# A seven-product block scheme in part of the down projections of a two-layer decoder trunk, on one core

## The chip, the core and the metric

The kernel runs on one core of a Trainium2 chip. The core has five engines that work side by side and meet only at semaphores: TensorE multiplies matrices (PE in the profile; PEld is its weight load), VectorE (DVE) and ScalarE (ACT) work elementwise, GpSimd (POOL) does some elementwise work, and SyncE (SP) starts the DMA transfers. Each engine takes its instructions in a fixed order, so an instruction that waits holds back all that stand behind it on the same engine. The metric is the time of one execution on the device, in microseconds (us), as a median over runs.

## The reference

The trunk has two residual layers, each a mixer and a gated MLP. Only the MLP (`conv_ffn`) matters here, and it runs twice:

```python
def conv_ffn(h, w_up, conv_w, conv_b, w_down):
    u = causal_dwconv(h @ w_up, conv_w, conv_b)
    gate, val = jnp.split(u, 2, axis=-1)
    return (jax.nn.silu(gate) * val) @ w_down
```

`h` is 512 tokens by 1024 channels, the inner width is 2816, all in float32. The down projection, `@ w_down`, is a product of 512 by 2816 with 2816 by 1024. Its result is added to the residual stream `x`.

## The kernel before

Activations lie transposed: channels on the 128 partitions, 512 tokens along the row. A float32 product is made of three products of a shorter float format (`F32R`): every operand is split into a high and a low part, and `products` (L155) issues, for each 128 by 128 block of weights, three matmuls of 512 columns into one PSUM bank: high by high (L159), high by low (L160), low by high (L161). Each matmul loads its 128 by 128 weights first (PEld).

`load` (L151) brings weights in: a DMA from SP's queue into a tile `raw`, ACT's copy into the high part `wh` (L139), DVE's subtraction into the low part `wl` (L144). Each of the three has three buffers, taken in turn. So a DMA waits until the `wl` of three loads earlier is made, and ACT's `wh` waits until TensorE is done with the load of three earlier.

`ffn` first runs the up projection (44 tiles; each ends in a few DVE and ACT operations, and the last of them is the low part `al` of the MLP's activation, L167), and keeps the activation as 22 tiles `ah` and `al` of 128 channels by 512 tokens. The down projection then makes the 8 output tiles one after another: for each `n`, three loads (8, 8 and 6 blocks of `k`), 66 matmuls, and `residual` (L217), in which DVE adds the bank to `x` (L219). In the first MLP, `residual` goes on with the next layer's norm (`Normed.add`: ACT's high part, DVE's low part, a square and a sum); in the second, it starts the DMA of the result. `Normed` keeps its parts in two large tiles, `xh` and `xl`, which the up projection reads.

The order on each engine is set by a scheduler when the program is built: it places the operations by its own estimate of when each can start, and the order is then fixed.

## Time and profile before

| what | value |
|---|---|
| median of 3 runs (lowest, highest) | 1125.85 us (1125.61, 1126.47) |
| the profiled execution's own time | 1128.6 us |
| its span, first to last instruction | 1126.8 us |
| granted clock of TensorE, mean | 0.988 of full speed |
| busy share of the span: PE, PEld, DVE, ACT, POOL | 97%, 78%, 66%, 45%, 14% |
| first down projection | 452.1 to 571.8 us of the span |
| second down projection | 1002.9 to 1122.6 us of the span |

The busy share counts any time in which an engine has an instruction under way. A matmul's duration covers its way through the pipeline, so matmuls overlap; what one costs in a row of many is the distance between two starts. Times in the rows further below are counted from the span's start.

### The profile page before, as it was taken

To read this page: it belongs to the slowest core of one execution; us is meant where nothing else is said; L and a number is where in the kernel's file an instruction comes from. 1 tells how busy PE (TensorE), PEld (TensorE's weight loads), DVE (VectorE), ACT (ScalarE), POOL (GpSimd) and SP (SyncE) were. 2 spreads that over 40 slices of the span, in tenths; PEclk is the share of its full clock that TensorE was granted. 3 is DMA by queue.
4 is the path that set the end of the run, shared out by engine and by line. 5 is a ranking of instruction groups with operands and counts; after the bars stand their busy time and mean duration, and the time that the engine had idled before them with its cause. 6 is when DMAs were issued, how large, how long until landed. Compare 5 with 4: busy or idle time off the path is not lost.

```text
span 1126.8 us, 12788 instructions
## 1 busy us (share of the span) xinstructions
PE 1089.6 (97%) x4898; PEld 875.4 (78%) x4898; DVE 748.7 (66%) x1052; ACT 508.0 (45%) x710; POOL 153.4 (14%) x131
## 2 busy tenths in 40 slices
PE   9989989999999999999999997799999999999998
PEld 7777767888888888888877762588888888888886
DVE  6888975677777777333369998776777777762221
ACT  6667644454444444322247444554444444441210
POOL 0132340000000000000039896000000000000000
PEclk9999999999999999999999998899999999999999
DMA  6311125223322223333334536132332233333340
GB/s 216 109 46 38 32 70 168 94 94 96 105 99 94 94 94 92 100 94 94 108 99 132 165 91 157 45 114 94 101 104 94 94 94 98 104 89 107 118 122 19
DMA packets 37406, 111.96 MB, mean 99 GB/s; under 512 B 4192, under 2 KB 4832, under 8 KB 37344
## 3 DMA queue, kind: packets, MB, share of 16 engines
q1 hardware_dynamic: 37344, 111.14, 32.0%
q8 instruction: 38, 0.62, 0.2%
q14 instruction: 24, 0.20, 0.1%
HBM read 107.18 MB, written 3.94 MB: 99 GB/s over the span
## 4 chain that ended last, share of the span: by engine, by line
PE 80%; DVE 9%; POOL 4%; ACT 3%; issue 2%; DMA 1%; SPq 0%; POOLq 0%; ACTq 0%; DVEq 0%
PE bank L159 25%; PE bank L161 25%; PE bank L160 25%; POOL y L754 3%; DVE bank L770 1%; ACT tap L751 1%; PE bank L724 1%; ACT wh L139 1%; DVE wl L144 1%; PE bank L894 1%; PE bank L895 1%; DVE u L696 1%; DMA stack<-d 1%; DVE fold L177 1%; DVE pl L167 0%
## 5 line engine op out<-in xcount | busy, mean ns | idle before, releaser
L159 PE MATMUL bank<-xh,wh 128*128 128x512 f32 x936 | 370.0, 396 | 1.6 <-ACT wh L257 1.5
L160 PE MATMUL bank<-xl,wh 128*128 128x512 f32 x936 | 366.2, 391 | 0.0
L161 PE MATMUL bank<-xh,wl 128*128 128x512 f32 x936 | 366.2, 391 | 0.0
L139 ACT ACTIVATE wh<-raw 128x1024 fp32r<-128x1024 f32 (+2 forms) x186 | 190.2, 1025 | 279.5 <-PE bank L160 236.7
L144 DVE TENSOR_TENSOR wl<-raw,wh 128x1024 fp32r<-128x1024 f32 (+2 forms) x175 | 210.6, 1205 | 143.8 <-ACT wh L139 141.9
L159 PEld LDWEIGHTS bank<-xh,wh 128*128 128x128 f32 x936 | 176.7, 189 | 42.6 <-issue 3.1
L161 PEld LDWEIGHTS bank<-xh,wl 128*128 128x128 f32 x936 | 176.3, 188 | 37.9 <-issue 0.7
L160 PEld LDWEIGHTS bank<-xl,wh 128*128 128x128 f32 x936 | 176.6, 189 | 36.8 <-issue 1.4
L159 PE MATMUL bank<-ah,wh 128*128 128x512 f32 x352 | 136.9, 389 | 0.0
L160 PE MATMUL bank<-al,wh 128*128 128x512 f32 x352 | 136.9, 389 | 0.0
L161 PE MATMUL bank<-ah,wl 128*128 128x512 f32 x352 | 136.9, 389 | 0.0
L931 DVE SCALAR_TENSOR_TENSOR y<-u,pt,y 128x511 f32<-128x511 f32 (+1 forms) x176 | 131.6, 748 | 7.7 <-ACT y L928 4.6
L926 DVE TENSOR_TENSOR u<-bank,rstd 128x512 f32<-128x512 f32 x88 | 60.5, 688 | 79.2 <-PE bank L161 79.2
L754 POOL TENSOR_TENSOR y<-y,tap 128x512 f32<-128x512 f32 x54 | 81.5, 1511 | 10.8 <-ACT tap L751 7.3
L166 ACT ACTIVATE ah<-y 128x512 fp32r<-128x512 f32 x44 | 27.8, 632 | 114.9 <-DVE y L936 114.9
L161 PEld LDWEIGHTS bank<-ah,wl 128*128 128x128 f32 x352 | 66.1, 188 | 13.8
L160 PEld LDWEIGHTS bank<-al,wh 128*128 128x128 f32 x352 | 66.1, 188 | 13.8
L159 PEld LDWEIGHTS bank<-ah,wh 128*128 128x128 f32 x352 | 66.1, 188 | 13.6
L928 ACT ACTIVATE y<-u,pt 128x512 f32<-128x512 f32 x88 | 71.3, 810 | 4.8 <-DVE u L926 3.8
L935 ACT ACTIVATE y<-y 128x512 f32<-128x512 f32 x44 | 27.8, 633 | 82.8 <-DVE y L931 82.8
L219 DVE TENSOR_TENSOR xr<-bank,xr 128x512 f32<-128x512 f32 x32 | 22.0, 690 | 63.0 <-PE bank L161 63.0
L770 DVE SCALAR_TENSOR_TENSOR bank<-u,pt,bank 128x512 f32<-128x512 f32 x79 | 56.8, 747 | 0.7
(194 smaller groups left out, 1072.5 us busy)
## 6 DMA issues: line engine op xcount, KB each, us to landing
raw<-in_w_up SPq DMA_DIRECT2D x88, 512.0 KB, 3.3
raw<-in_w_down SPq DMA_DIRECT2D x32, 512.0 KB, 3.5
raw<-in_w_pw SPq DMA_DIRECT2D x24, 512.0 KB, 3.4
stack<-d SPq DMA_DIRECT2D x28, 256.0 KB, 5.1
raw<-in_w_down SPq DMA_DIRECT2D x16, 384.0 KB, 3.2
xr<-in_x SPq DMA_DIRECT2D x16, 256.0 KB, 5.4
raw<-in_w_out SPq DMA_DIRECT2D x8, 512.0 KB, 3.6
raw<-in_w_qk SPq DMA_DIRECT2D x6, 512.0 KB, 3.4
```

The source lines that it names most:

```text
L139: S.activation(out=wh, in_=raw, func=AF.Copy)
L144: on.tensor_tensor(out=wl, in0=raw, in1=wh.bitcast(F32), op=ALU.subtract)
L159: PE.matmul(acc, lhsT=ah, rhs=bh, start=(first and i == 0), stop=False)
L160: PE.matmul(acc, lhsT=ah, rhs=bl, start=False, stop=False)
L161: PE.matmul(acc, lhsT=al, rhs=bh, start=False, stop=(last and i == n - 1))
L166: S.activation(out=h, in_=src, func=AF.Copy)
L754: G.tensor_tensor(out=mine["y2"], in0=mine["y2"], in1=mine[s], op=ALU.add)
L770: V.scalar_tensor_tensor(out=acc, in0=shifted(s), scalar=wcol(s), in1=acc, op0=ALU.mult, op1=ALU.add)
L926: V.tensor_tensor(out=u, in0=acc, in1=nrm.r, op=ALU.mult)
L928: S.activation(out=y, in_=u, func=AF.Identity, scale=col("cv_w", 3 * ct + 2), bias=col("cv_b", ct))
L931: V.scalar_tensor_tensor(out=y[:, s:], in0=u[:, 0:T - s], scalar=col("cv_w", 3 * ct + 2 - s), in1=y[:, s:], op0=ALU.mult, op1=ALU.add)
L935: S.activation(out=ys[0], in_=ys[0], func=AF.Silu)
```

## The change

Four blocks of weights, two neighbouring `k` and two neighbouring outputs `n`, form a 2 by 2 block matrix; the two `k` tiles of the activation, cut into two halves of 256 tokens, form another. Their product takes eight block products of 256 columns in the plain way. The change makes it of seven (Winograd's form of Strassen's scheme), from sums and differences of the blocks. It does so for the first six of the eleven pairs of `k`, and not for every pair of outputs: `USED` says that output pairs 0 to 3 use it for 2, 4, 6 and 6 pairs of `k`, so 18 of the 44 in each down projection. The rest (`plain`) is as before, in loads of 2, 4, 6 or 8 blocks.

- `differences(f)`, once for each of the six pairs of `k`: GpSimd adds the high and low parts of two activation tiles back together (L971, twice), DVE makes four half-width sums and differences (L973 to L976), and ACT and DVE split them (L166, L167 on 1024 columns). They share one tile `r`, of which there is one buffer. Four of the results lie in the space of `xh` and `xl`, two in a new tile.
- `fast(p, f, ...)`: a DMA of four blocks, three DVE operations for four more (L985, L987, L988), the split of seven blocks (896 columns: L139, L144), and 21 matmuls of 256 columns, into the two banks of the outputs and two more, `e`.
- `combine(p, e)`: once for each pair of outputs, ACT and DVE work out what the banks `e` add to the two outputs (L1017 to L1029), in a tile `qd` that takes the same single buffer as `r`.
- In each pair of outputs the loads stand in this order: plain ones, the fast ones, `combine`, differences still to be made, the last plain ones, the additions to `x` (L1060). Three differences are made ahead of output pair 0, two behind its `combine`, and one behind that of pair 1. The next norm takes its first six tiles when the fourth fast product of the last pair is done.

The core of the diff (`up` holds the up projection as it was):

```diff
+    FAST = tuple(range(6))
+    USED = (2, 4, 6, 6)
+    HT = T // 2
+    halves = [slice(0, HT), slice(HT, T)]
     def ffn(layer, nrm, next_norm):
-        with tc.tile_pool(name="ffn", bufs=1) as fp, tc.tile_pool(name="ffn2", bufs=2) as f2:
+        with tc.tile_pool(name="ffn", bufs=1) as fp:
             ah = fp.tile([P, FT, T], F32R, name="ah")
             al = fp.tile([P, FT, T], F32R, name="al")
...
-            nxt = next_norm(f2)
-            for n in range(KT):
+            with tc.tile_pool(name="ffn2", bufs=2) as f2:
+                up(layer, nrm, ah, al, f2)
+            with tc.tile_pool(name="ffnt", bufs=1) as ft:
+                return down(layer, ah, al, ft, next_norm)
...
-                for k0 in range(0, FT, KT):
-                    kk = min(KT, FT - k0)
-                    wh, wl = load(w_down[layer, n][:, k0:k0 + kk], [kk, P])
-                    products(acc, [(wh[:, k], wl[:, k], ah[:, k0 + k], al[:, k0 + k])
-                                   for k in range(kk)], first=(k0 == 0), last=(k0 + kk == FT))
-                residual(acc, n, nxt)
-            if nxt is not None:
-                nxt.finish()
-            return nxt
...
+    def down(layer, ah, al, ft, next_norm):
+        near = [per.tile([P, 4, 4, HT], F32R, tag=t, name=f"t_{t}") for t in ("xh", "xl")]
+        far = [ft.tile([P, 2, 4, HT], F32R, name=f"t_far{i}") for i in range(2)]
+        parts_of = [[t[:, f] for t in near] if f < 4 else [t[:, f - 4] for t in far]
+                    for f in range(len(FAST))]
+        def differences(f):
+            k = 2 * FAST[f]
+            r = ft.tile([P, 6, HT], F32, tag="r", name="r")
+            flat = r.rearrange("p a t -> p (a t)")
+            for i, on in ((0, G), (1, G)):
+                on.tensor_tensor(out=flat[:, i * T:(i + 1) * T], in0=ah[:, k + i].bitcast(F32),
+                                 in1=al[:, k + i].bitcast(F32), op=ALU.add)
+            V.tensor_tensor(out=r[:, 4:6], in0=r[:, 0:1].to_broadcast([P, 2, HT]), in1=r[:, 1:3],
+                            op=ALU.subtract)
+            V.tensor_tensor(out=r[:, 2], in0=r[:, 2], in1=r[:, 4], op=ALU.subtract)
+            V.tensor_tensor(out=r[:, 3], in0=r[:, 3], in1=r[:, 2], op=ALU.subtract)
+            split(r[:, 2:6], *parts_of[f])
+        def fast(p, f, o, e, first_e, last_e):
+            j = FAST[f]
+            raw = wp.tile([P, 8, P], F32, tag="wr", name="raw", bufs=3)
+            nc.sync.dma_start(out=raw[:, 0:4].rearrange("p (n k) c -> p n k c", n=2),
+                              in_=w_down[layer, 2 * p:2 * p + 2, :, 2 * j:2 * j + 2].rearrange(
+                                  "n p k c -> p n k c"))
+            V.tensor_tensor(out=raw[:, 4:6], in0=raw[:, 0:1].to_broadcast([P, 2, P]),
+                            in1=raw[:, 1:3], op=ALU.add)
+            V.tensor_tensor(out=raw[:, 6], in0=raw[:, 4], in1=raw[:, 2], op=ALU.add)
+            V.tensor_tensor(out=raw[:, 7], in0=raw[:, 6], in1=raw[:, 3], op=ALU.add)
+            wh, wl = load_parts(raw[:, 1:8], [7, P])
+            th, tl = parts_of[f]
+            def b(k, half):
+                return ah[:, 2 * j + k, halves[half]], al[:, 2 * j + k, halves[half]]
+            def t(i):
+                return th[:, i], tl[:, i]
+            for i, (bh, bl), acc, half in (
+                    (1, b(0, 1), e[0], 0), (5, t(0), e[0], 1), (3, t(2), e[1], 0),
+                    (4, t(3), e[1], 1), (6, b(1, 0), o[1], 0), (2, b(1, 1), o[1], 1),
+                    (0, t(1), o[0], 1)):
+                products(acc[:, halves[half]], [(wh[:, i], wl[:, i], bh, bl)],
+                         first_e and i in (1, 3), last_e and i in (5, 4))
+        def plain(p, ks, o, first, last):
+            for n in range(2):
+                w = load(w_down[layer, 2 * p + n][:, ks[0]:ks[-1] + 1], [len(ks), P])
+                products(o[n], [(w[0][:, i], w[1][:, i], ah[:, k], al[:, k])
+                                for i, k in enumerate(ks)], first, last)
+        def combine(p, e):
+            x0, x1 = res["x"][:, 2 * p], res["x"][:, 2 * p + 1]
+            r = ft.tile([P, 6, HT], F32, tag="r", name="qd")
+            q, d = r[:, 0:2].rearrange("p a t -> p (a t)"), r[:, 2:4]
+            S.activation(out=q[:, halves[0]], in_=e[0][:, halves[0]], func=AF.Copy)
+            V.tensor_tensor(out=q[:, halves[1]], in0=e[0][:, halves[1]], in1=q[:, halves[0]],
+                            op=ALU.subtract)
+            V.tensor_tensor(out=d, in0=e[1].rearrange("p (a t) -> p a t", a=2),
+                            in1=q[:, halves[1]].rearrange("p (a t) -> p a t", a=1).to_broadcast(
+                                [P, 2, HT]), op=ALU.add)
+            V.tensor_tensor(out=x1[:, halves[1]], in0=x1[:, halves[1]], in1=q[:, halves[0]],
+                            op=ALU.add)
+            V.tensor_tensor(out=x1[:, halves[0]], in0=x1[:, halves[0]], in1=d[:, 0],
+                            op=ALU.subtract)
+            x0h = x0.rearrange("p (a t) -> p a t", a=2)
+            V.tensor_tensor(out=x0h, in0=x0h, in1=d[:, 1:2].to_broadcast([P, 2, HT]), op=ALU.add)
+            V.tensor_tensor(out=x0[:, halves[0]], in0=e[1][:, halves[0]], in1=x0[:, halves[0]],
+                            op=ALU.add)
+        for f in range(USED[0] + 1):
+            differences(f)
+        nxt, made, todo = None, USED[0] + 1, []
+        for p in range(KT // 2):
+            o = [bank(next(turn)) for _ in range(2)]
+            e = [bank(next(turn)) for _ in range(2)]
+            use = list(range(USED[p]))
+            ks = [k for k in range(FT) if k // 2 not in [FAST[f] for f in use]]
+            cuts = ((0, 8, 14, 18), (0, 6, 14), (0, 2, 10), (0, 2, 10))[p]
+            blocks = [ks[a:b] for a, b in zip(cuts, cuts[1:])]
+            for i, ks in enumerate(blocks[:-1]):
+                plain(p, ks, o, i == 0, False)
+            for f in use:
+                fast(p, f, o, e, f == 0, f == use[-1])
+                if p == KT // 2 - 1 and f == 3:
+                    nxt = next_norm and next_norm()
+                    for n in range(2 * p if nxt else 0):
+                        nxt.add(n)
+            combine(p, e)
+            if made < len(FAST) and p < 2:
+                to = (USED[1] + 1, len(FAST))[p]
+                for f in range(made, to):
+                    differences(f)
+                made = to
+            plain(p, blocks[-1], o, False, True)
+            for n in range(2 * p, 2 * p + 2):
+                xn = res["x"][:, n]
+                V.tensor_tensor(out=xn, in0=o[n % 2], in1=xn, op=ALU.add)
+                if next_norm is None:
+                    nc.sync.dma_start(out=out[:, n], in_=xn)
+                elif nxt is not None:
+                    nxt.add(n)
+        if nxt is not None:
+            nxt.finish()
+        return nxt
```

On TensorE a load of 8 blocks of one output reads, in the order before, as three matmuls for each `k` (`ah`, `al`: the activation; `wh`, `wl`: the weights):

```order
L159 MATMUL bank<-ah,wh 128x512
L160 MATMUL bank<-al,wh 128x512
L161 MATMUL bank<-ah,wl 128x512
L159 MATMUL bank<-ah,wh 128x512
L160 MATMUL bank<-al,wh 128x512
L161 MATMUL bank<-ah,wl 128x512
```

The same engine now, at the end of the first fast product of a pair (`t_xh`, `t_xl` are the parts of the differences):

```order
L159 MATMUL bank<-t_xh,wh 128x256
L160 MATMUL bank<-t_xl,wh 128x256
L161 MATMUL bank<-t_xh,wl 128x256
L159 MATMUL bank<-ah,wh 128x256
L160 MATMUL bank<-al,wh 128x256
L161 MATMUL bank<-ah,wl 128x256
L159 MATMUL bank<-ah,wh 128x256
L160 MATMUL bank<-al,wh 128x256
L161 MATMUL bank<-ah,wl 128x256
L159 MATMUL bank<-t_xh,wh 128x256
L160 MATMUL bank<-t_xl,wh 128x256
L161 MATMUL bank<-t_xh,wl 128x256
```

So 12 matmuls of 512 columns have become 21 of 256, each with a weight load of its own.

On DVE, at the seam of the first up and down projection, the order before was this (`u`, `y`, `al`: the end of the up projection; `wl`: low parts of weights for the down projection):

```order
L926 TENSOR_TENSOR u_3745<-bank_3720,rstd_1803 128x512
L144 TENSOR_TENSOR wl_3824<-raw_3820,wh_3822 128x768
L931 SCALAR_TENSOR_TENSOR y_3747<-u_3745,pt_67,y_3747 128x511
L931 SCALAR_TENSOR_TENSOR y_3747<-u_3745,pt_67,y_3747 128x510
L936 TENSOR_TENSOR y_3710<-y_3710,y_3747 128x512
L167 TENSOR_TENSOR al_2038<-y_3710,ah_2037 128x512
L144 TENSOR_TENSOR wl_3853<-raw_3849,wh_3851 128x1024
L144 TENSOR_TENSOR wl_3883<-raw_3879,wh_3881 128x1024
L219 TENSOR_TENSOR xr_1791<-bank_3759,xr_1791 128x512
```

And now, from the same place on (`raw` of 256 or 128 columns: the sums of weights; `r`, `t_xl`: the first differences; 896 columns: the low parts of a fast product's weights):

```order
L956 TENSOR_TENSOR y_3710<-y_3710,y_3747 128x512
L985 TENSOR_TENSOR raw_3929<-raw_3929 128x256
L167 TENSOR_TENSOR al_2035<-y_3710,ah_2034 128x512
L987 TENSOR_TENSOR raw_3929<-raw_3929 128x128
L988 TENSOR_TENSOR raw_3929<-raw_3929 128x128
L144 TENSOR_TENSOR wl_3879<-raw_3875,wh_3877 128x768
L973 TENSOR_TENSOR r_3763<-r_3763 128x512
L975 TENSOR_TENSOR r_3763<-r_3763 128x256
L976 TENSOR_TENSOR r_3763<-r_3763 128x256
L167 TENSOR_TENSOR t_xl_3760<-r_3763,t_xh_3759 128x1024
L144 TENSOR_TENSOR wl_3906<-raw_3899,wh_3904 128x896
L973 TENSOR_TENSOR r_3771<-r_3771 128x512
```

The differences stand in the same queue as the low parts of the weights; POOL's two additions for each stand in POOL's own queue, the first behind the `al` shown here.

The third place is DVE ahead of the first fast product of output pair 1, where there was only the plain sequence of `wl` and `xr`:

```order
L144 TENSOR_TENSOR wl_4053<-raw_4049,wh_4051 128x768
L976 TENSOR_TENSOR r_3967<-r_3967 128x256
L985 TENSOR_TENSOR raw_4073<-raw_4073 128x256
L985 TENSOR_TENSOR raw_4103<-raw_4103 128x256
L1060 TENSOR_TENSOR xr_1791<-bank_3788,xr_1791 128x512
L167 TENSOR_TENSOR t_xl_3760<-r_3967,t_xh_3759 128x1024
```

```order
L987 TENSOR_TENSOR raw_4103<-raw_4103 128x128
L988 TENSOR_TENSOR raw_4073<-raw_4073 128x128
L988 TENSOR_TENSOR raw_4103<-raw_4103 128x128
L985 TENSOR_TENSOR raw_4133<-raw_4133 128x256
L973 TENSOR_TENSOR r_3975<-r_3975 128x512
L144 TENSOR_TENSOR wl_4080<-raw_4073,wh_4078 128x896
```

The fifth differences (`r_3975`, not needed before output pair 2) stand ahead of `wl_4080`, the low parts of the weights of pair 1's first fast product.

## Rows read from the trace of the kernel before

**Rows 1.** Two down projections by stage: busy time (and instructions) of each engine, PEclk.

```profile
452.10:571.80 119.70, 119.70 (x530) 99.10 (x528) 43.64 (x49) 33.96 (x41) 0.00 (x0) 1.00 0.32 95
1002.90:1122.60 119.70, 119.70 (x529) 98.89 (x527) 32.95 (x34) 23.04 (x24) 0.00 (x0) 1.00 0.30 92
```

**Rows 2.** Timeline of PE at two 256-column triples of the attention.

```profile
81.84 0.28 PE L159 MATMUL bank<-ph,vhl 128*128 128x256 f32 x1
...
82.20 0.22 PE L159 MATMUL bank<-ph,vhl 128*128 128x128 f32 x1
...
145.70 0.28 PE L159 MATMUL bank<-ph,vhl 128*128 128x256 f32 x1
...
146.05 0.22 PE L159 MATMUL bank<-ph,vhl 128*128 128x128 f32 x1
```

**Rows 3.** Groups of DVE, shapes apart: busy, mean ns, idle before.

```profile
L144 DVE TENSOR_TENSOR wl<-raw,wh 128x1024 fp32r<-128x1024 f32 x155 | 192.6, 1245 | 143.8 <-ACT wh L139 141.9
L144 DVE TENSOR_TENSOR wl<-raw,wh 128x768 fp32r<-128x768 f32 x16 | 15.3, 959 | 0.0
L219 DVE TENSOR_TENSOR xr<-bank,xr 128x512 f32<-128x512 f32 x32 | 22.0, 690 | 63.0 <-PE bank L161 63.0
L167 DVE TENSOR_TENSOR pl<-bank,ph 128x256 fp32r<-128x256 f32 x8 | 3.3, 411 | 0.0
L167 DVE TENSOR_TENSOR pl<-bank,ph 128x128 fp32r<-128x128 f32 x8 | 2.3, 284 | 0.7 <-ACT ph L166 0.7
```

**Rows 4.** Groups of ACT, shapes apart.

```profile
L139 ACT ACTIVATE wh<-raw 128x1024 fp32r<-128x1024 f32 x166 | 175.4, 1060 | 233.7 <-PE bank L160 191.1 <-issue 33.7 <-PE bank L898 5.1
L166 ACT ACTIVATE ph<-bank 128x256 fp32r<-128x256 f32 x8 | 3.0, 376 | 1.0 <-PE bank L534 0.9
```

**Rows 5.** Timeline of DVE at the end of the first up projection.

```profile
455.46 0.69 DVE L936 TENSOR_TENSOR y<-y 128x512 f32<-128x512 f32 x1
456.86 0.69 DVE L167 TENSOR_TENSOR al<-y,ah 128x512 fp32r<-128x512 f32 x1 [0.70 <-ACT ah L166]
```

**Rows 6.** POOL's additions of 512 columns, by line and tile: min, median, max ns.

```profile
L754 POOL TENSOR_TENSOR y<-y,tap x54: 1264/1298/2375, 590.1 to 692.1; 128x512 f32<-128x512 f32 x54
L422 POOL TENSOR_TENSOR us<-us x6: 1039/1040/1277, 139.0 to 160.9; 128x512 f32<-128x512 f32 x6
```

**Rows 7.** DVE and POOL at the same time: timelines of two stretches, and line L696.

```profile
598.09 2.09 DVE L144 TENSOR_TENSOR wl<-raw,wh 128x1024 fp32r<-128x1024 f32 x1 [0.64 <-ACT wh L139]
599.18 3.86 POOL L754 TENSOR_TENSOR y<-y,tap 128x512 f32<-128x512 f32 x2
601.81 0.74 DVE L770 SCALAR_TENSOR_TENSOR bank<-u,pt,bank 128x512 f32<-128x512 f32 x1
...
146.11 2.79 POOL L144 TENSOR_TENSOR wl<-raw,wh 128x1024 fp32r<-128x1024 f32 x1
146.69 2.23 DVE L429 TENSOR_TENSOR mx<-us,pt 128x7 f32<-128x7 f32 x1
...
L696 DVE TENSOR_TENSOR u<-ab x8: 692/1772/1784, 587.8 to 681.7; 128x512 f32<-128x512 f32 x8
```

**Rows 8.** DMA issues: KB each, us from issue to landing.

```profile
raw<-in_w_down SPq DMA_DIRECT2D x16, 384.0 KB, 3.2
...
w<-in_w_dw SPq DMA_DIRECT2D x1, 128.0 KB, 2.3
```

**Rows 9.** A standstill of PE and the stretch after it: timeline, then its window.

```profile
73.18 0.66 PE L534 MATMUL bank<-ident,p 128*128 128x128 f32 x2 [2.73 <-DVE p L526]
...
74.07 0.63 PE L160 MATMUL bank<-xl,wh 128*128 128x512 f32 x1
74.50 0.63 PE L161 MATMUL bank<-xh,wl 128*128 128x512 f32 x1
...
73.20:76.60 3.40, 3.40 (x10) 2.78 (x11) 3.27 (x8) 2.94 (x7) 0.00 (x0) 0.53 0.00 0
```

More of the change, by code (lines that the diff above doesn't have):

```diff
@@ L910, in odd_layer @@
             return nxt
+    FAST = tuple(range(6))
+    USED = (2, 4, 6, 6)
+    HT = T // 2
+    halves = [slice(0, HT), slice(HT, T)]
     def ffn(layer, nrm, next_norm):
-        with tc.tile_pool(name="ffn", bufs=1) as fp, tc.tile_pool(name="ffn2", bufs=2) as f2:
+        with tc.tile_pool(name="ffn", bufs=1) as fp:
             ah = fp.tile([P, FT, T], F32R, name="ah")
             al = fp.tile([P, FT, T], F32R, name="al")
-            for i in range(FT):
-                ys = []
-                for j in range(2):
-                    wh, wl = load(w_up[layer, 2 * i + j], [KT, P])
-                    acc = bank(next(turn))
-                    products(acc, [(wh[:, k], wl[:, k], nrm.h[:, k], nrm.l[:, k])
-                                   for k in range(KT)])
-                    ct = layer * 2 * FT + j * FT + i
-                    u = f2.tile([P, T], F32, tag="tt", name="u")
-                    V.tensor_tensor(out=u, in0=acc, in1=nrm.r, op=ALU.mult)
-                    y = f2.tile([P, T], F32, tag=f"y{j}", name="y")
-                    S.activation(out=y, in_=u, func=AF.Identity, scale=col("cv_w", 3 * ct + 2),
-                                 bias=col("cv_b", ct))
-                    for s in (1, 2):
-                        V.scalar_tensor_tensor(out=y[:, s:], in0=u[:, 0:T - s],
-                                               scalar=col("cv_w", 3 * ct + 2 - s), in1=y[:, s:],
-                                               op0=ALU.mult, op1=ALU.add)
-                    ys.append(y)
-                S.activation(out=ys[0], in_=ys[0], func=AF.Silu)
-                V.tensor_tensor(out=ys[0], in0=ys[0], in1=ys[1], op=ALU.mult)
-                split(ys[0], ah[:, i], al[:, i])
-            nxt = next_norm(f2)
-            for n in range(KT):
-                acc = bank(next(turn))
-                for k0 in range(0, FT, KT):
-                    kk = min(KT, FT - k0)
-                    wh, wl = load(w_down[layer, n][:, k0:k0 + kk], [kk, P])
-                    products(acc, [(wh[:, k], wl[:, k], ah[:, k0 + k], al[:, k0 + k])
-                                   for k in range(kk)], first=(k0 == 0), last=(k0 + kk == FT))
-                residual(acc, n, nxt)
-            if nxt is not None:
-                nxt.finish()
-            return nxt
@@ new lines, in ffn, with up @@
+            with tc.tile_pool(name="ffn2", bufs=2) as f2:
+                up(layer, nrm, ah, al, f2)
+            with tc.tile_pool(name="ffnt", bufs=1) as ft:
+                return down(layer, ah, al, ft, next_norm)
+    def up(layer, nrm, ah, al, f2):
+        for i in range(FT):
+            ys = []
+            for j in range(2):
+                wh, wl = load(w_up[layer, 2 * i + j], [KT, P])
+                acc = bank(next(turn))
+                products(acc, [(wh[:, k], wl[:, k], nrm.h[:, k], nrm.l[:, k])
+                               for k in range(KT)])
+                ct = layer * 2 * FT + j * FT + i
+                u = f2.tile([P, T], F32, tag="tt", name="u")
+                V.tensor_tensor(out=u, in0=acc, in1=nrm.r, op=ALU.mult)
+                y = f2.tile([P, T], F32, tag=f"y{j}", name="y")
+                S.activation(out=y, in_=u, func=AF.Identity, scale=col("cv_w", 3 * ct + 2),
+                             bias=col("cv_b", ct))
+                for s in (1, 2):
+                    V.scalar_tensor_tensor(out=y[:, s:], in0=u[:, 0:T - s],
+                                           scalar=col("cv_w", 3 * ct + 2 - s), in1=y[:, s:],
+                                           op0=ALU.mult, op1=ALU.add)
+                ys.append(y)
+            S.activation(out=ys[0], in_=ys[0], func=AF.Silu)
+            V.tensor_tensor(out=ys[0], in0=ys[0], in1=ys[1], op=ALU.mult)
+            split(ys[0], ah[:, i], al[:, i])
```

4 lines of the change are left out of this document (2 added, 2 removed).

## The prediction

> **What bounds the kernel now.** I read the page first: TensorE is busy for 97% of the span. Then the two stages that are changed: each down projection takes 119.7 us, TensorE is busy in all of it at the full clock, DVE in 43.6 and 33.0 us, ACT in 34.0 and 23.0, POOL in none [rows 1]. The stage is 8 outputs by 22 blocks by 3 matmuls, 528, so a matmul of 512 columns costs 119.7 / 528 = 0.2267 us from start to start (its duration says nothing, as matmuls overlap). The reader is to see that nothing but the matmuls sets the end here: less matmul time is less time, and any wait that the change brings to TensorE is lost in full, since TensorE has no slack to make it up.
>
> The sum is made against the profiled execution, 1128.6 us with a span of 1126.8. It lies 2.75 us above the median of the runs, 1125.85, so I add the same difference to the median.
>
> **What the half-width matmuls save.** In the attention, 256-column matmuls with a weight load each follow one another: three take 82.20 - 81.84 = 0.36 us in one place and 146.05 - 145.70 = 0.35 in another [rows 2], 0.118 each. That is a little more than half of 0.2267. A fast product takes 21 x 0.118 = 2.48 us in place of 12 x 0.2267 = 2.72, and saves 0.24 us, not an eighth. 18 of them save 4.3 us in a down projection, 8.7 in both. This term holds as far as the short triples stand for long runs.
>
> **What is added elsewhere.** DVE: a fast product needs sums of 256, 128 and 128 columns and a low part of 896, which lies between the rows of 768 and 1024 (0.96 and 1.25), about 1.1. With 0.41 and 0.28 for the sums [rows 3] that is 2.1 us, against about 0.6 for the four blocks before. The differences cost 0.69 + 0.41 + 0.41 and a low part of 1.25, 2.8 us, six times; `combine` about 3.0, four times. In all DVE gets some 18 x 1.5 + 17 + 12 = 56 us more and comes to about 100 of 120. ACT gets about 16 more (copies of 896 and 1024 columns at up to 1.06, of 256 at 0.38 [rows 4]). POOL gets 12 additions. No engine is filled on average, so what matters is the order: what each low part of the weights stands behind in DVE's queue.
>
> **The chain through the single buffer.** All differences and `combine` share one buffer, so they run strictly one behind the other. A round is two POOL additions, three DVE operations, ACT's copy of 1024 columns, DVE's low part.
> - POOL: an addition of 512 columns takes 1.30 at the median; one form took 1.04 [rows 6]. L971 reads two different tiles, as L754 does, so I take 1.29. Two are 2.58.
> - DVE 0.69 + 0.41 + 0.41, ACT 1.06, DVE 1.25 [rows 3, 4]. Handing over between engines costs about 0.04: the row that ends at 456.15 is followed by a copy of 0.63 and a row that starts at 456.86 [rows 5]. Six times are 0.24. Sum: 6.6 us.
> - To this comes a collision. While POOL adds, a DVE low part of 1024 columns took 2.09 instead of 1.25, L696 at the median 1.77 instead of 0.69, and a DVE operation on 7 columns 2.23; two POOL additions took 3.86 instead of 2.6. DVE's L770, which has a bank among its operands, took its plain 0.74 meanwhile [rows 7]. So when both read two SBUF tiles, one waits for the other's instruction to end. In the new order, the low part of a fast or plain load stands right at POOL's first addition in rounds 2, 3 and 4 and starts first: POOL waits 0.9. Rounds 2 and 3 become 7.5, round 1 (a sum of 128 columns) 6.9.
>
> No row shows the added DVE forms beside POOL. The Trainium skill (GPSIMD Engine Reference, section 1, Specifications) says that POOL shares its SBUF interfaces with VectorE and contends with DVE instructions that have two SBUF inputs, which L973 to L988 all have. By the rule these all collide; if only the forms of the rows did, the waits below would be about 1 us less in each down projection, and the forecast 2 us less.
>
> Now the times, from the first matmul of the down projection at 0 (452.1 of the span). TensorE wants: pair 0's plain loads to 14 x 2 x 0.68 = 19.0, two fast products to 24.0, the last plain ones to 29.4, pair 1's first plain ones to 37.6, and then its first fast product, whose low part is due at its third matmul, at 37.8.
> - The last `al` of the up projection was done at 457.55 [rows 5], 5.4; a sum of weights now stands ahead of it (0.41). POOL waits for it: the rounds start at 5.8 and end at 12.7, 20.2 and 27.7.
> - The low part of pair 0's last plain load stands behind the third DVE operation of round 3 (27.7 - 1.25 - 1.06 - 0.1 = 25.3) and is done at 26.0; it is due at 24.5. TensorE waits 1.5.
> - `combine` follows round 3: one more low part (0.69), then 0.41 + 0.41 + 0.69 + 0.41 + 0.69 before the buffer is free, at 31.0.
> - Round 4: POOL to 34.5; three DVE operations with an addition to `x` and a low part of 768 columns between them (0.69 + 0.96), to 37.7; ACT and the low part to 40.0. The low part of 768 costs TensorE a further wait inside this stretch.
> - Round 5's additions, with small sums of weights between them, end at about 42.9. Behind them in DVE's queue stand the rest of the sums, L973 and only then pair 1's first fast low part: about 45.0. Due at 37.8, so TensorE has by then lost 7 us in all.
> - Behind this, pair 1's third and fourth fast product wait for raw tiles that were freed late (a DMA of 256 KB lands in 2.3 to 3.2 us, between the rows of 128 and 384 KB [rows 8]; I take 2.6): 0.5. In pair 2, round 6 delays a low part, and so a DMA, once more: about 0.8. Pair 3 has no round ahead of it and no wait.
>
> That is 8.3 us of waits against 4.3 saved: +4.0 for each down projection. The second has the same order of differences on DVE, with the result's DMAs among SP's raw loads; a raw load held behind one of them is due ten us later, so I cost it at nothing (about 1 us, the third fast product of a pair, if the DMA lands late).
>
> **Costed at nothing.** The six norm steps that wait for the fourth fast product of the last pair lie beside 10.9 us of plain matmuls; the steps that end the stage are the same as before. If ACT's six copies stood ahead of a weight's high part, up to 6 x 1.06 = 6.4 us would show there.
>
> **The clock.** A standstill of 2.73 us was followed by 3.4 us at half the clock (512-column matmuls 0.43 apart, granted 0.53 [rows 9]), which cost 1.6. Ahead of pair 1's fast products TensorE stands still for some 3 to 4 us at a stretch. I count 1 us over both, since DVE catches up meanwhile. Bounds: 0 and 3.2.
>
> Sum: 1128.6 + 8 + 1 = 1137.6 for the profiled execution, 1134.8 for the median; I say 1134.5.
>
> **Rivals.**
> - *Faster: the rounds are quick enough.* With POOL at 1.04 and no collision, the rounds shrink by 0.8, 1.4, 1.4, 1.4 and 0.8, 5.8 in all; pair 1's first fast low part comes at 39.2, the waits are some 2.3, and 2 us stay saved in each: 1121.9. With no wait at all it would be 1117.1. It decides where the five rounds together are 4 us shorter than I have them. For it: 1.04 is in the trace. Against: none of L754's 54 took less than 1.26 [rows 6]. 15%.
> - *No change: the waits eat what is saved.* Half of those 4 us: 1124 to 1128. 17%.
> - *Slower still:* DMAs at 3.2 (some 2.5 us more in each), half the clock in both: 1139 to 1145. 10%.
> - *The matmuls don't run at 0.118 in long runs*, being held by their weight loads: each 0.01 us costs 7.6, partly inside the waits; from 0.130 on nothing is saved. Six spacings of six speak against it. 3%, on the slow side.
> - My forecast, 1129 to 1139: 55%.
>
> **Numbers.** Median 1134.5 us. From 1122 to 1140: that leaves out most of the first rival's best case and half of the two slow ones, about 2 in 10. The likeliest case alone is 1129 to 1139. A measurement of this kernel can tell 0.2% (2.3 us) from no change: faster 0.15, same 0.17, slower 0.68 (forecast, slower still, and the slow matmuls).
>
> **What the profile after would show.** PE: 256-column matmuls 0.118 apart in the fast products; if 0.11, the saving is larger and TensorE only waits longer. POOL: 12 additions in each down projection, many over 1.3 us. PE's waits: one of 1 to 2 us ahead of pair 0's last plain load, 3 to 5 us ahead of pair 1's first fast product, on DVE's `wl` and ACT's `wh`; a granted clock of half behind it. Each stage about 123 to 125 us in place of 119.7. I am wrong if POOL's additions take 1.0, if DVE's operations don't wait for them, or if the `al` that starts the rounds comes much earlier.

## The result and the profile after

The changed kernel takes 1139.38 us (median of 4 runs, 1137.83 to 1139.65), the one before beside it 1125.73 (4 runs, 1124.27 to 1126.47): a ratio of 1.012, 95% interval 1.0102 to 1.0138. It is slower by 13.65 us where I had forecast 8.65. Its profiled execution took 1137.83 us with a span of 1136.1 (1128.6 and 1126.8 before).

The windows of the two down projections of the changed kernel; they answer to [rows 1]:

```profile
core 0: us, PE busy (x) PEld busy (x) DVE busy (x) ACT busy (x) POOL busy (x), PEclk, DMA share, GB/s
450.37:575.81 125.44, 119.42 (x692) 105.23 (x691) 98.32 (x163) 48.16 (x62) 17.58 (x12) 0.99 0.32 95
1006.26:1132.17 125.91, 119.51 (x691) 105.07 (x689) 88.10 (x148) 37.94 (x46) 17.57 (x12) 0.99 0.31 90
```

Each stage is longer, by 5.74 and 6.21 us, 12 in all, and TensorE, which filled it before, now stands idle for 6 us of it. The rest of the span is 2.7 us shorter. Of this, 1.7 lie ahead of the first down projection, where before's profile had a stretch of half clock (granted 0.79 in 173 to 181), which this one lacks (1.00 there); what made up the other 1.0 stays open.

What TensorE waits for in the first of the two stages, from the view of waits:

```profile
PE bank L161 <- DVE wl L144: 3.3, 5, 1.6
PE bank L159 <- ACT wh L139: 2.7, 1, 2.7
```

TensorE's timeline at the longest of these waits, ahead of pair 1's first fast product; the bracket is the idle time before a row and what ended it:

```profile
491.00 0.39 PE L160 MATMUL bank<-al,wh 128*128 128x512 f32 x1
491.23 0.39 PE L161 MATMUL bank<-ah,wl 128*128 128x512 f32 x1
494.34 0.38 PE L159 MATMUL bank<-ah,wh 128*128 128x256 f32 x1 [2.73 <-ACT wh L139]
494.57 0.28 PE L160 MATMUL bank<-al,wh 128*128 128x256 f32 x1
495.47 0.39 PE L161 MATMUL bank<-ah,wl 128*128 128x256 f32 x1 [0.63 <-DVE wl L144]
495.69 0.28 PE L159 MATMUL bank<-t_xh,wh 128*128 128x256 f32 x1
...
497.69 0.41 PE L160 MATMUL bank<-al,wh 128*128 128x256 f32 x1
497.90 0.41 PE L161 MATMUL bank<-ah,wl 128*128 128x256 f32 x1
...
499.34 0.28 PE L159 MATMUL bank<-ah,wh 128*128 128x256 f32 x1
499.46 0.28 PE L160 MATMUL bank<-al,wh 128*128 128x256 f32 x1
499.58 0.28 PE L161 MATMUL bank<-ah,wl 128*128 128x256 f32 x1
```

The reader is to see three things. The product starts 2.9 us late (counted from start to start, over the usual spacing), and its low part comes another 0.8 late. Behind the standstill the starts are 0.21 us apart instead of 0.12: the granted clock is 0.51 in 495.9 to 499.3, and 0.50 in the same place of the second stage. And at the full clock 256 columns cost 0.120, not 0.118.

POOL's timeline in the first part of the stage: the additions of five rounds, two to a row.

```profile
456.67 2.58 POOL L971 TENSOR_TENSOR r<-ah,al 128x512 f32<-128x512 f32 x2 [281.64 <-DVE al L167]
464.10 3.31 POOL L971 TENSOR_TENSOR r<-ah,al 128x512 f32<-128x512 f32 x2 [4.85 <-DVE t_xl L167]
471.55 3.31 POOL L971 TENSOR_TENSOR r<-ah,al 128x512 f32<-128x512 f32 x2 [4.13 <-DVE t_xl L167]
482.01 3.10 POOL L971 TENSOR_TENSOR r<-ah,al 128x512 f32<-128x512 f32 x2 [7.15 <-DVE xr L1028]
490.47 2.55 POOL L971 TENSOR_TENSOR r<-ah,al 128x512 f32<-128x512 f32 x2 [5.36 <-DVE t_xl L167]
```

Each round starts when the one before has made its low part (`t_xl`), and the fourth when `combine` is done (L1028): 6.3, 13.7, 21.2, 31.6 and 40.1 us into the stage. On DVE, rounds 2 to 4 each bring a gap of 2 us and more, in which DVE waits for POOL's additions at L973, and what stands behind L973 in its queue waits too:

```profile
471.38 1.08 DVE L144 TENSOR_TENSOR wl<-raw,wh 128x896 fp32r<-128x896 f32 x1
474.89 0.69 DVE L973 TENSOR_TENSOR r<-r 128x512 f32<-128x512 f32 x1 [2.42 <-POOL r L971]
475.62 0.43 DVE L975 TENSOR_TENSOR r<-r 128x256 f32<-128x256 f32 x1
476.08 0.42 DVE L976 TENSOR_TENSOR r<-r 128x256 f32<-128x256 f32 x1
476.42 0.68 DVE L144 TENSOR_TENSOR wl<-raw,wh 128x512 fp32r<-128x512 f32 x1
...
490.31 1.59 DVE L987 TENSOR_TENSOR raw<-raw 128x128 f32<-128x128 f32 x2
491.82 1.55 DVE L988 TENSOR_TENSOR raw<-raw 128x128 f32<-128x128 f32 x2
493.30 0.41 DVE L985 TENSOR_TENSOR raw<-raw 128x256 f32<-128x256 f32 x1
493.63 0.68 DVE L973 TENSOR_TENSOR r<-r 128x512 f32<-128x512 f32 x1
494.32 1.09 DVE L144 TENSOR_TENSOR wl<-raw,wh 128x896 fp32r<-128x896 f32 x1
```

The low part at 476.42 is that of pair 0's last plain load; it costs TensorE 1.8 us from start to start (the longest of the five waits on `wl`, 1.6 by the view, which counts from the end of the matmul before). That at 494.32 belongs to pair 1's first fast product and ends 45.0 us into the stage. Ahead of it two pairs of sums of 128 columns take 1.59 and 1.55 in place of 0.56: POOL's additions of round 5 hold each of them up by 1 us.

The long standstill itself is a wait for the high part (`wh`), which ACT can only make when the last of these sums is done:

```profile
493.34 1.79 ACT L139 ACTIVATE wh<-raw 128x896 fp32r<-128x896 f32 x2 [3.43 <-DVE raw L988]
```

So what holds pair 1's first fast product is this: its sums stand behind round 4's low part in DVE's queue, collide with round 5's additions, and ACT's copy follows them. L973 of round 5, which also stands ahead of the low part, ends at 494.31, when that copy (0.95 long) ends too, and so adds nothing.

### The profile page after: what moved, and what is told of

It is laid out like the page before. It is cut to its first block, busy times and chain, and to the rows that moved or that the text cites. A ratio compares the mean times of both kernels' runs of the same rounds, so it can differ in the third digit from the quotient of the medians.

```text
span 1136.1 us, 13895 instructions
## 1 busy us (share of the span) xinstructions
PE 1086.5 (96%) x5222; PEld 886.2 (78%) x5222; DVE 858.9 (76%) x1280; ACT 536.8 (47%) x754; POOL 189.2 (17%) x155
## 5 line engine op out<-in xcount | busy, mean ns | idle before, releaser
L139 ACT ACTIVATE wh<-raw 128x1024 fp32r<-128x1024 f32 (+5 forms) x210 | 205.4, 985 | 205.8 <-PE bank L160 134.4
L144 DVE TENSOR_TENSOR wl<-raw,wh 128x1024 fp32r<-128x1024 f32 (+4 forms) x199 | 231.6, 1169 | 42.1 <-ACT wh L139 39.8
L971 POOL TENSOR_TENSOR r<-ah,al 128x512 f32<-128x512 f32 x24 | 35.2, 1484 | 664.3 <-PE bank L161 306.7
L161 PE MATMUL bank<-ah,wl 128*128 128x512 f32 (+1 forms) x316 | 113.5, 359 | 7.0 <-DVE wl L144 7.0
L159 PE MATMUL bank<-ah,wh 128*128 128x512 f32 (+1 forms) x316 | 112.5, 356 | 5.4 <-ACT wh L139 5.4
L160 PE MATMUL bank<-al,wh 128*128 128x512 f32 (+1 forms) x316 | 112.2, 355 | 0.0
L754 POOL TENSOR_TENSOR y<-y,tap 128x512 f32<-128x512 f32 x54 | 81.5, 1511 | 10.7 <-ACT tap L751 7.3
L166 ACT ACTIVATE ah<-y 128x512 fp32r<-128x512 f32 x44 | 27.8, 632 | 114.9 <-DVE y L956 114.9
L161 PEld LDWEIGHTS bank<-ah,wl 128*128 128x128 f32 x316 | 60.4, 191 | 18.5 <-DVE wl L144 10.5
L159 PEld LDWEIGHTS bank<-ah,wh 128*128 128x128 f32 x316 | 60.5, 191 | 14.3 <-ACT wh L139 6.3
L160 PEld LDWEIGHTS bank<-al,wh 128*128 128x128 f32 x316 | 60.5, 191 | 8.1
```

What stands on the lines that cost most here:

```text
L139: S.activation(out=wh, in_=raw, func=AF.Copy)
L144: on.tensor_tensor(out=wl, in0=raw, in1=wh.bitcast(F32), op=ALU.subtract)
L159: PE.matmul(acc, lhsT=ah, rhs=bh, start=(first and i == 0), stop=False)
L160: PE.matmul(acc, lhsT=ah, rhs=bl, start=False, stop=False)
L161: PE.matmul(acc, lhsT=al, rhs=bh, start=False, stop=(last and i == n - 1))
L166: S.activation(out=h, in_=src, func=AF.Copy)
```

## The experiments

My theory: TensorE waits because the rounds of differences run one behind the other through a single buffer, each is 7.4 us long with POOL's additions in it, and DVE's queue holds the low parts of the weights behind them. Rivals: the half-width matmuls are what costs; DVE simply has too much to do; the collisions of POOL and DVE cost by themselves, wherever they lie. All ratios are to the kernel before, run beside them on the same chip.

**1. The half-width matmuls alone**, in the kernel before:

```diff
...
+                        if k0 + k < 9:
+                            for h in (slice(0, T // 2), slice(T // 2, T)):
+                                products(acc[:, h], [(wh[:, k], wl[:, k], ah[:, k0 + k, h], al[:, k0 + k, h])],
+                                         first=(k0 + k == 0 and h.start == 0), last=False)
...
```

> The kernel before, with nothing of the scheme: only the matmuls of the first 9 of the 22 blocks of each output run as two of 256 columns in place of one of 512 (72 blocks in each down projection, 6 matmuls for 3). It prices the half-width matmul in long runs. At 0.118 a block takes 0.708 us for 0.680, 144 blocks cost +4.0: about 1129.8. At 0.120, as the trace of the changed kernel has it, 0.720 for 0.680, +5.8: about 1131.5. If half width costs just half (0.1133), nothing: 1125.7.

Measured: 1133.09 us, ratio 1.0049 (1.0034 to 1.0065). Both stages are filled to the end:

```profile
452.20:574.92 122.72, 122.72 (x745) 110.38 (x744) 43.62 (x49) 33.91 (x41) 0.00 (x0) 1.00 0.31 93
1006.43:1129.15 122.72, 122.72 (x745) 110.19 (x743) 32.93 (x34) 23.04 (x24) 0.00 (x0) 1.00 0.30 90
```

3.02 us more for 432 matmuls in place of 216: (3.02 + 216 x 0.2267) / 432 = 0.1203 each. The price of the trace holds. A fast product takes 21 x 0.120 = 2.52 us for 2.72, and saves 0.20, 3.6 in a stage. So half-width matmuls save less than I had counted, but they don't make the change slower.

**2. One round of differences only.**

```diff
         def differences(f):
+            if f > 0:
+                return
...
-            th, tl = parts_of[f]
+            th, tl = parts_of[0]
```

> The changed kernel with the first round of differences alone; all fast products multiply with the first round's differences, so the values of 15 of 18 of them are those of another block. The matmuls, the weights' sums and combine stay as they are. If the chain of rounds makes the waits (my theory), 7 us of waits and 1.7 of half clock go from each down projection, and the stage is 116 to 117 us: about 1120 to 1122. If it is the fast products' own sums and low parts on DVE, or raw tiles that come late, most of the waits stay: 1133 to 1139.

Measured: 1119.42 us, ratio 0.9932 (0.9912 to 0.9952). No wait of TensorE is left in either stage:

```profile
450.54:566.71 116.17, 116.17 (x692) 103.91 (x691) 82.05 (x142) 43.58 (x57) 2.59 (x2) 1.00 0.35 102
999.44:1115.60 116.16, 116.16 (x691) 103.72 (x689) 72.89 (x128) 33.41 (x41) 2.60 (x2) 1.00 0.33 98
```

Without rounds 2 to 6, the weights' own sums, their raw tiles and `combine` cost TensorE nothing: the whole loss comes with these rounds. The stage without waits is 3.5 us shorter than before's 119.70, which is what the seven products save.

**3. Both additions on DVE.**

```diff
-            for i, on in ((0, G), (1, G)):
+            for i, on in ((0, V), (1, V)):
```

> The changed kernel with both additions of each round on DVE in place of POOL. POOL is idle, so nothing collides; a round takes 2 x 0.69 + 1.5 + 1.06 + 1.25 + 0.2 = 5.4 us in place of 7.5, five rounds are some 9 us shorter, and pair 1's first fast low part comes at 36, before it is due at 37.8. DVE gets 8 us more, some 107 of 125. My theory (chain length and collision): waits of at most 1 us in each down projection and no half clock, about 1120 to 1124. Rival (DVE has too much to do in the first 40 us, so it is its work and not POOL's pace): the waits stay, 1136 to 1142.

Measured: 1119.79 us, ratio 0.9942 (0.9923 to 0.996): the change with this edit is faster than the kernel before. The stages take 116.92 and 116.86 us with DVE at 99 and 89 us of them, the rounds start 6.20 apart, and pair 1's first fast low part is done 36.9 us into the stage. DVE has 12 additions more to do than in the changed kernel, and TensorE hardly waits: so DVE was not too full.

**4. A buffer of its own for combine.**

```diff
-            r = ft.tile([P, 6, HT], F32, tag="r", name="qd")
-            q, d = r[:, 0:2].rearrange("p a t -> p (a t)"), r[:, 2:4]
+            if p == 3:
+                r = ft.tile([P, 6, HT], F32, tag="r", name="qd")
+                q, d = r[:, 0:2].rearrange("p a t -> p (a t)"), r[:, 2:4]
+            else:
+                q = per.tile([P, T], F32, tag="rstd", name="q2")
+                d = per.tile([P, T], F32, tag="ssum", name="d2").rearrange("p (a t) -> p a t", a=2)
```

> The changed kernel with two tiles of its own for q and d of combine in the first three pairs, so that round 4's additions wait for round 3's low part only, and no longer for combine. If the single buffer is what holds round 4 (my theory), POOL starts it some 3 us sooner, pair 1's first fast low part comes some 3 us sooner, and the waits fall from 7 to about 4 in each down projection: about 1133, or 1130 if the half clock goes with the long standstill. Rival (round 4 is held by DVE's queue and by the collisions, not by the buffer): 1138 to 1140.

Measured: 1138.21 us, ratio 1.01 (1.0083 to 1.0116): a miss, nothing is won. POOL's and DVE's timelines of it:

```profile
478.99 3.11 POOL L971 TENSOR_TENSOR r<-ah,al 128x512 f32<-128x512 f32 x2 [4.13 <-DVE t_xl L167]
```

```profile
479.43 0.42 DVE L1022 TENSOR_TENSOR q<-bank,q 128x256 f32<-128x256 f32 x1
479.76 1.18 DVE L1027 TENSOR_TENSOR xr<-xr,q 128x256 f32<-128x256 f32 x1
480.87 0.68 DVE L1024 TENSOR_TENSOR d<-bank,q 128x512 f32<-128x512 f32 x1
482.13 0.69 DVE L973 TENSOR_TENSOR r<-r 128x512 f32<-128x512 f32 x1 [0.59 <-POOL r L971]
...
484.68 0.95 DVE L144 TENSOR_TENSOR wl<-raw,wh 128x768 fp32r<-128x768 f32 x1
```

The buffer did hold POOL: round 4 starts 3.02 us sooner, as expected. But the scheduler then put round 4's operations ahead of pair 1's plain low part, which was made at 481.76 in the changed kernel and now at 484.68; it costs TensorE 2.9 us there, the longest wait of the stage. So what was wrong was that the wait would shrink with an earlier round: it moved to another load in the same queue. All waits of the first stage together did fall by 1.1 us, from 7.0 to 5.9. But behind this one the clock stayed at half until 491.8 (granted 0.51 in 485.9 to 491.9, matmuls of 512 columns 0.43 apart), which cost some 2.8 us where the stretch of the changed kernel cost 1.5. The run changed the order along with the buffer, and doesn't price the buffer alone.

**5. The fifth round moved behind the second pair's combine.**

```diff
-                to = (USED[1] + 1, len(FAST))[p]
+                to = (USED[1], len(FAST))[p]
```

> The changed kernel with the fifth round of differences moved in program order from behind the first pair's combine to behind the second pair's; its result is first needed by the third pair. Additions stay on POOL, the buffer stays single. My theory: pair 1's first fast product waits because its sums and low part stand behind round 5 in DVE's queue and its raw tile is freed late; with round 5 gone from there its wait of 2.9 us and the 0.8 behind it go, and with the long standstill the half clock (1.5); rounds 5 and 6 cost the third pair up to 1 us. Some 4 to 5 us less in each down projection: 1129 to 1132. Rival (DVE is too full in this stretch and the wait only moves on): 1136 to 1140.

Measured: 1141.46 us, ratio 1.0144 (1.0129 to 1.0159): my expectation missed, and the rival's direction was right. The wait ahead of pair 1's first fast product did fall, from 2.9 to 0.7 us, with no half clock behind it (granted 1.00 in 493 to 500); the 0.8 behind it stayed. The two pairs of sums ahead of it, free of round 5's additions, took 0.49 each in place of 1.59 and 1.55: 2.2 us, so that most of the longest wait in the changed kernel was this collision. But rounds 5 and 6 now follow each other ahead of pair 2's fast products, and one of 3.8 us stands there:

```profile
489.78 0.49 DVE L987 TENSOR_TENSOR raw<-raw 128x128 f32<-128x128 f32 x2
490.19 0.49 DVE L988 TENSOR_TENSOR raw<-raw 128x128 f32<-128x128 f32 x2
...
512.36 1.23 DVE L167 TENSOR_TENSOR t_far<-r,t_far 128x1024 fp32r<-128x1024 f32 x1
513.50 0.68 DVE L207 TENSOR_TENSOR ssum<-ssum,sq 128x512 f32<-128x512 f32 x1
516.61 0.69 DVE L973 TENSOR_TENSOR r<-r 128x512 f32<-128x512 f32 x1 [2.43 <-POOL r L971]
...
519.23 1.08 DVE L144 TENSOR_TENSOR wl<-raw,wh 128x896 fp32r<-128x896 f32 x1
```

Moving a round moves its gap on DVE to whatever low part stands behind it next. Experiments 4 and 5 agree in this: neither of the two places tried made the kernel quicker.

**6. Unneeded additions on POOL, beside the sums on DVE** (the edit of 3, and in each round):

```diff
+            spare = per.tile([P, T], F32, tag="rstd", name="spare")
+            for i in range(2):
+                if f == 0:
+                    sides = [s[:, k + i] for s in (ah, al)]
+                else:
+                    sides = [s[:, 2 * i:2 * i + 2].rearrange("p a t -> p (a t)") for s in parts_of[f - 1]]
+                G.tensor_tensor(out=spare, in0=sides[0].bitcast(F32),
+                                in1=sides[1].bitcast(F32), op=ALU.add)
```

> The version with both additions of each round on DVE (1119.8 us), with two unneeded additions of 512 columns on POOL for each round, released when the round before ends, so at about the times at which the changed kernel's additions ran; nobody waits for them. It has the collisions of POOL with DVE without POOL in the chain. If the chain's length through POOL makes the waits and a collision only delays single DVE instructions by up to 1.3 us: 1120 to 1124. If the collisions themselves hold DVE back enough (12 in a stage, each up to 1.3 us twice): 1128 to 1136.

Measured: 1139.48 us, ratio 1.0123 (1.0108 to 1.0139). All that experiment 3 had won is gone again, beyond both of the ranges, and without POOL in the chain. DVE's timeline shows how, beside POOL's third and fourth pairs of additions (472.30 to 475.71, 480.15 to 483.20):

```profile
472.19 2.39 DVE L979 TENSOR_TENSOR r<-ah,al 128x512 f32<-128x512 f32 x2
474.62 1.64 DVE L981 TENSOR_TENSOR r<-r 128x512 f32<-128x512 f32 x1
...
480.53 0.42 DVE L1026 TENSOR_TENSOR qd<-bank,qd 128x256 f32<-128x256 f32 x1
480.86 1.18 DVE L1031 TENSOR_TENSOR xr<-xr,qd 128x256 f32<-128x256 f32 x1
481.97 0.68 DVE L1028 TENSOR_TENSOR qd<-bank,qd 128x512 f32<-128x512 f32 x1
482.57 1.45 DVE L144 TENSOR_TENSOR wl<-raw,wh 128x768 fp32r<-128x768 f32 x1
```

The two sums take 2.39 for 1.28 and the operation behind them 1.64 for 0.69: the collisions stretch DVE's own part of the round, and the third round starts 8.40 us behind the second (463.79 and 472.19, against 6.20 in experiment 3). They also stretch low parts of weights directly (1.45 above, where 768 columns take 0.95). So the collisions alone cost as much as POOL's additions in the chain; how much of it came through the chain, and how much through low parts stretched directly, this run doesn't tell apart.

**7. A third addition on POOL in each round.**

```diff
-            for i, on in ((0, G), (1, G)):
+            for i, on in ((0, G), (1, G), (2, G)):
...
-                                 in1=al[:, k + i].bitcast(F32), op=ALU.add)
+                                 in1=al[:, k + i % 2].bitcast(F32), op=ALU.add)
```

> The changed kernel with a third, unneeded addition of 512 columns on POOL in each round, whose result the round's first DVE operation overwrites; so each round is 1.3 us longer on POOL, and DVE has nothing more to do. My theory: five rounds stand ahead of pair 1's first fast low part, so it comes some 5 x 1.3 = 6.5 us later, and the waits go from 7 to about 13 in each down projection: about 1152. Rival (DVE's own work sets the pace, POOL is beside the point): 1138 to 1142.

Measured: 1152.21 us, ratio 1.0235 (1.022 to 1.0251), on the figure of my theory. The rounds start 8.70 apart (464.91 - 456.21), and the first stage is 131.90 us, 15.7 above the one without waits, where the changed kernel has 9.3: 6.4 more, 5 x 1.3.

**8. Copies on POOL in place of the additions.**

```diff
-                on.tensor_tensor(out=flat[:, i * T:(i + 1) * T], in0=ah[:, k + i].bitcast(F32),
-                                 in1=al[:, k + i].bitcast(F32), op=ALU.add)
+                on.tensor_copy(out=flat[:, i * T:(i + 1) * T], in_=ah[:, k + i].bitcast(F32))
```

> The changed kernel with each addition on POOL replaced by a copy of the high part alone, so the low parts are left out of the differences. POOL then reads one SBUF tile and not two. It is to show whether a POOL instruction with one SBUF input also has to wait for DVE's and holds DVE up, and whether it is shorter than 1.29 us. If a copy takes 1.29 and collides like an addition: 1138 to 1140, rounds of 7.4 us. If it does not collide: rounds of 6.7, about 1133 to 1135. If it is also shorter (below 0.8 us): rounds below 5.8 and waits nearly gone, 1120 to 1125.

Measured: 1121.4 us, ratio 0.9958 (0.9944 to 0.9971). POOL's timeline:

```profile
455.99 1.23 POOL L971 COPY r<-ah 128x512 f32<-128x512 f32 x2 [281.64 <-DVE al L167]
462.05 1.97 POOL L971 COPY r<-ah 128x512 f32<-128x512 f32 x2 [4.83 <-DVE t_xl L167]
468.14 1.97 POOL L971 COPY r<-ah 128x512 f32<-128x512 f32 x2 [4.12 <-DVE t_xl L167]
```

A copy takes 0.61 for an addition's 1.29, and collides just as much: the second and third pair take 1.97 for 1.23, the same 0.74 that the additions lose. With rounds of 6.1 us in place of 7.4 the waits are nearly gone (one of 0.4 us is left in the first stage), though the copies collide.

**9. Unneeded additions on POOL in the kernel before.**

```diff
+                    if n < 2:
+                        spare = per.tile([P, 4, P], F32, tag="spare", name="spare")
+                        for i in range(2):
+                            G.tensor_tensor(out=spare, in0=wh[:, 0:4].bitcast(F32),
+                                            in1=wl[:, 0:4].bitcast(F32), op=ALU.add)
```

> The kernel before with 12 unneeded additions of 512 columns on POOL in each down projection, two behind each of the first six loads of weights, reading that load's high and low part; nobody waits for them. DVE has 44 of 120 us to do there. If a collision costs TensorE only where DVE has no slack (as I read the run with unneeded additions beside the sums on DVE, which lost all that the sums on DVE had won): no change, 1125 to 1128. If additions on POOL cost time by themselves, wherever they lie: 1130 to 1138.

Measured: 1126.66 us, ratio 1.0005 (0.9994 to 1.0015): no change. They do collide (a low part of 1024 columns at 462.28 takes 2.23 us, not 1.23), but the first stage is 119.69 us and TensorE busy in all of it:

```profile
450.28:569.97 119.69, 119.69 (x530) 99.14 (x529) 48.36 (x50) 34.24 (x42) 13.45 (x10) 1.00 0.33 99
```

A collision alone is free while DVE has slack, and no low part is late. This speaks against collisions as a cost of their own, wherever they lie.

**10. One addition on each engine.**

```diff
-            for i, on in ((0, G), (1, G)):
+            for i, on in ((0, G), (1, V)):
```

> The changed kernel with the second addition of each round on DVE and the first still on POOL. The two read two SBUF tiles each, so one waits for the other: 0.69 + 1.29 = 2.0 us in place of 2.6 to 3.3, a round some 1.3 us shorter, five rounds 6.5. By the chain's length: pair 1's first fast low part at 38.5, due at 37.8, waits of 1 to 2 us in each stage, 1120 to 1124. If it is the collisions that count (there are as many as before): 1130 to 1138.

Measured: 1130.1 us, ratio 1.0043 (1.0024 to 1.0061), at the lower edge of the second expectation, and above the first. The rounds start 6.76 apart, and not 6.1: POOL's addition takes 1.73 to 2.01 in each of the first five rounds, where 1.28 is its time without a collision (round 6). A wait of 2.0 us stays at pair 1's first fast product, and a stretch of half clock follows it (granted 0.50 in 491.2 to 494.6).

The runs side by side, first stage; the distance is that from the first round's start to the second's:

| kernel | distance of rounds, us | pair 1's first fast low part done at | stage, us | median, us |
|---|---|---|---|---|
| third addition (7) | 8.70 | 47.5 (other order) | 131.90 | 1152.21 |
| changed kernel | 7.43 | 45.0 | 125.44 | 1139.38 |
| one on each (10) | 6.76 | 41.1 | 122.19 | 1130.1 |
| both on DVE (3) | 6.20 | 36.9 | 116.92 | 1119.79 |
| copies (8) | 6.06 | 38.3 | 117.18 | 1121.4 |
| one round only (2) | - | - | 116.17 | 1119.42 |

From 7.43 to 8.70 a microsecond in the round is worth 6.46 / 1.27 = 5.1 us in the stage, about one for each of the five rounds ahead of pair 1's fast products; from 6.76 to 7.43 it is 4.9. Below 6.2 there is nothing left to win, since the low part is done by the time it is due (37.8 by the prediction's count) or soon after. Experiments 4 to 6 don't lie on this line: their first stages took 125.62, 126.61 and 126.57 us, with pair 1's first fast low part done at 44.5, 42.9 and 44.1, because their waits lie at other loads as well.

## Why the prediction was right

**The forecast, slower, and its cause stand.** The median lies 4.9 us above the forecast and inside the range, but only by 0.6 us; it lies 0.4 above the likeliest case (1129 to 1139), where the rival "slower still" begins.

**What the half-width matmuls save** was sized too high: 0.120 and not 0.118 in long runs, 3.5 us in a stage (experiment 2) and not 4.3. The short triples of [rows 2] were 2% too quick for a run of 21. Its rival, with its break-even at 0.130, did not come.

**The chain.** The forecast of the rounds' starts was 5.8, 12.7, 20.2 and 31.0 for the fourth; they came at 6.3, 13.7, 21.2 and 31.6. Pair 1's first fast low part was put at 45.0 and came at 45.0. The first round was 7.4 and not 6.9 long, as the first low part collided too (2.03 for 0.95 at 458.03). The collisions cost POOL 0.73 in rounds 2 and 3, where I had 0.9. That 45.0 was met so exactly is in part luck: the rounds were 1.0 us late at the third, and `combine` (2.9 for 3.3) and round 4 (8.4 for 9.0) won that back. The last link was not quite the one named: the prediction had the low part behind L973, and it was the collided sums and ACT's copy that held the product. The Trainium skill (GPSIMD Engine Reference, section 1, Specifications) says that POOL contends with DVE instructions that have two SBUF inputs. The trace agrees: in experiment 6 the two DVE operations that read a bank took 0.42 and 0.68 beside POOL, and those of two SBUF inputs between and behind them 1.18 for 0.41 and 1.45 for 0.95.

**The waits**: 8.3 in each stage by the forecast. The stages are 125.44 - 116.17 = 9.27 and 9.75 us over the one without waits; 1.5 of each is half clock (some 16 matmuls at 0.2135 for 0.120), which leaves 7.8 and 8.2. The main places were those forecast: 1.8 at pair 0's last plain load (forecast 1.5), 0.7 at a plain load of pair 1 (forecast without a figure of its own), 2.9 and 0.8 at pair 1's first fast product, and in pair 2 0.4 in the first stage and 0.9 in the second (0.8). The 0.5 for late raw tiles in pair 1 did not come, and 0.4 at pair 0's second fast product was not forecast.

**The clock** was sized too low: I counted 1 us over both, where the one row bore out 1.6 for each [rows 9]. Both stages had their stretch, 3.0 us in all. That catching up would spare one of them did not come.

So the two stages together cost 12.0 us where I had 9: 1.6 more for the matmuls, 2.0 more for the clock, 0.6 less for the waits. That the profiled execution came at 1137.83 all the same, against 1137.6, is luck: the rest of its span was 2.7 us shorter than before's, most of it by the stretch of half clock that it lacked. That is why the median missed by more: I took before's offset of 2.75 us off, while the profiled execution of after is the quickest of its four, 1.55 below their median. Where those 1.55 us lie no trace shows.

**The rivals.** "The rounds are quick enough" needed 4 us less over five rounds. Experiments 3 and 8 made them 6 to 7 shorter and got 1119.8 and 1121.4, where the rival had 1121.9. So its condition was right and not met: none of POOL's 24 additions took less than 1.28 us, as none of L754's had taken less than 1.26 [rows 6]. "No change" needed them 2 us shorter, and pair 1's first fast low part came as late as forecast. "Slower still" is met by its figure, at its lower edge (1139), and by one of its two conditions: the half clock came in both stages, but the late DMAs did not (256 KB landed in 2.8 us at the median in the first stage, where it had 3.2 and I had 2.6).

What stays open: how much of the loss the single buffer is worth alone (experiment 4 moved the order as well), how the loss divides between the length of the rounds and the collisions (the collisions bring it about with POOL out of the chain, experiment 6, and shorter rounds do away with it though POOL still collides, experiment 8), and a version with POOL's pace but without collisions, which wasn't tried.

## What to carry to other kernels

Before work is given to an idle engine, look whether its result stands in a chain that runs several times ahead of a due time: a microsecond there counted five times, and the busy engine that was twice as quick (0.69 for 1.29) was the better place, even at 85% busy. Where an in-order engine waits in the middle of its queue, moving the wait only changes who stands behind it (experiments 4 and 5); shortening it helps. A collision of two engines is free where both have slack (9), and twelve additions on POOL in each stage cost all that had been won where DVE's results were awaited (6).

## What the runs showed of the hardware

- **Half the columns cost more than half.** At the full clock 512 columns take 0.2267 us and 256 take 0.120; at half clock 256 take 0.2135, which is 256 columns at 1.2 GHz. At 2.4 GHz the columns alone would be 0.2133 and 0.1067, so at the full clock each matmul of these runs, with a weight load of its own, carries 0.013 us beside its columns; at half clock nothing is left over. What the 0.013 us are, no run here shows. Nine more matmuls for each fast product eat 0.12 of the 0.32 us that its columns save.
- **The first matmul behind a wait takes longer**: at 494.34, 495.47 and 477.16 the next start follows 0.10 us later than it does in a run (0.23 for 0.12, 0.34 for 0.23), and so behind each of the six waits of the first stage.
- **POOL's copies wait for DVE like its additions do**, though they read one SBUF tile (experiment 8; a pair 1.97 for 1.23), so two inputs on POOL's side are not needed for it; they take 0.61 us, as DVE's additions of this size take 0.69.
- **POOL can stand behind several DVE instructions**: the fifth pair of unneeded additions in experiment 6 took 6.76 us in place of 2.6, its first addition alone 4.66, as DVE's operations of two SBUF inputs came one behind the other (3.71 for the pair in the same place of the second stage). So these two engines do not meet at semaphores alone.
